# The one added to the decay's tanh in the RWKV projections: from VectorE's instruction to a second ScalarE activation in place

## The chip, the cores and the metric

The kernel runs on one core of a Trainium2 chip. The metric is the device time of one execution in microseconds (us), as the median of several runs. TensorE (PE, with its weight loads PEld), VectorE (DVE), ScalarE (ACT), GpSimd (POOL) and the DMA queues issued by SyncE (SP) work side by side; each engine runs its own instructions strictly in the order in which they stand in its list.

## The reference, cut to what matters

One layer of a hybrid encoder, 2048 tokens of 1024 numbers. The token mixer has attention heads and bidirectional RWKV heads over one shared projection, and then 16 experts follow. The piece that the change touches is the decay `w` of the RWKV heads, for each of two directions:

```
p = _centred_shift(p, mu_shift)
r, k, v, dw, da, dg = jnp.split(p, ...)
tw = jnp.tanh(dw)
...
w = jnp.exp(-DECAY_SCALE * jax.nn.sigmoid(w0[d] + tw @ w_up[d]))
a = jax.nn.sigmoid(a0[d] + da @ a_up[d])
kd = heads(k * (1.0 + (a - 1.0) * k_a))
```

The kernel has no sigmoid: it uses sigmoid(z) = (tanh(z/2) + 1)/2. So the logarithm of the decay needs `u = tanh(z/2) + 1`, and the running sums of `u` over chunks of tokens give all decay products.

## The kernel before, in words

The program has three stages: projections (`phase1`, to about 760 us), the mixers (RWKV and attention as two interleaved streams, to about 2250 us), and the output projection with the experts (to the end).

`phase1` works through two halves of 1024 tokens. In each half, a hand-written order calls pieces: four `heads(ct)` pieces h0 to h3 (128 RWKV channels each), four query/key pieces q0 to q3, one value piece, and, in the first half, the early loading of the next half's x. A heads piece projects r, k and v by `shifted`, and then `prep` makes what the mixers need of them.

- `project` makes one product: 24 matmuls (L247) of 258 columns into one PSUM bank of a pool `p1_pj` with 3 banks. `shifted` follows it with ACT's first tap (L263) and two DVE taps (L265) that add the left and right neighbours. PE gets the bank back only when the second DVE tap is done.
- `prep` goes over 2 stretches of 512 tokens and 2 directions d, that is 32 times in the whole of `phase1`. Each time: PE's low-rank products (L385), ACT's tanh `u` (L388) and tanh `a` (L389), **the one that is added to `u` (L390)**, DVE's scan `cum` (L392), exponentials on ACT (L394, L404 to L406), and products on DVE and POOL (L397 to L416) into a tile `X` that goes out by DMA. `a` and `u` have one buffer each, so the next tanh `a` (L389) waits until DVE's L414 has read the last one.
- `load_piece` prepares x for the projections: DVE copies `ht` (L195), and `split` (ACT L148, DVE or POOL L149) divides it into the two parts `hh` and `hl`. The query/key pieces put L324 to L329 on DVE.

The order of instructions on each engine is not written by hand below the level of pieces: the framework's scheduler places all instructions of all pieces by its own planned times, with `high_priority` for the taps. An instruction that is put on another engine can therefore move others, up to the mixers.

Of the kernel before, what the change touches and what calls it, by code (L numbers as in the profile page):

```python
# [11 lines left out]
AF = mybir.ActivationFunctionType  # L12
ALU = mybir.AluOpType
# [24 lines left out]
class Encoder:  # L38
# [317 lines left out]
    def prep(self, half, ct, rkv, lora, rates, sg):  # L356

        nc, ps, tpool = self.nc, self.ps, self.tpool
        tt, ts, stt, act = nc.vector.tensor_tensor, nc.vector.tensor_scalar, nc.vector.scalar_tensor_tensor, nc.scalar.activation
# [9 lines left out]
        for q in range(2):  # L369
            qs = slice(q * 512, (q + 1) * 512)  # L370
            t0 = half * HT + q * 512
            c0 = t0 // CH
            r, k, v = rkv[0][q], rkv[1][q], rkv[2][q]
            tl = lambda tag, bufs=None: tpool.tile([P, 512], F32, tag=tag, name=tag, bufs=bufs)
            self.to_tokens(v, self.d_v[t0 : t0 + 512, cs_])
            pb = self.spread(rt, q)
            kk = tl("kkn", 2)
            stt(out=kk, in0=k, scalar=self.kkh[:, ct : ct + 1], in1=pb, op0=ALU.mult, op1=ALU.mult)
            kds = []
            for d in range(2):  # L380
                pp = []
                for m in range(2):
                    pm = ps.tile([P, 512], F32, tag="ps", name="lora_ps")
                    for i in range(2):
                        nc.tensor.matmul(pm, lora[m][i][:, d, :], rates[m][:, qs], start=(i == 0), stop=(i == 1))  # L385
                    pp.append(pm)
                u, a = tl("u"), tl("a")
                act(out=u, in_=pp[0], func=AF.Tanh, bias=self.w0h[:, 4 * d + ct : 4 * d + ct + 1], scale=0.5)  # L388
                act(out=a, in_=pp[1], func=AF.Tanh, bias=self.a0h[:, 4 * d + ct : 4 * d + ct + 1], scale=0.5)  # L389
                nc.vector.tensor_scalar(out=u, in0=u, scalar1=1.0, scalar2=None, op0=ALU.add)  # L390
                cum = tl("cum")
                nc.vector.tensor_tensor_scan(out=cum, data0=self.cmask, data1=u, initial=0.0, op0=ALU.mult, op1=ALU.add)  # L392
                last = c3(cum)[:, :, CH - 1 : CH]
                act(out=self.pc[:, d, ct, c0 : c0 + 8], in_=last.rearrange("p c o -> p (c o)"), func=AF.Exp, scale=-0.5 * DSC)  # L394
                ex = tl("ex")
                if d == 0:
                    tt(out=ex, in0=cum, in1=u, op=ALU.subtract)  # L397
                    inc = cum
                else:
                    tt(out=c3(ex), in0=last.to_broadcast([P, 8, CH]), in1=c3(cum), op=ALU.subtract)  # L400
                    inc = u
                    tt(out=inc, in0=ex, in1=u, op=ALU.add)
                pinv = tl("pinv")
                act(out=pinv, in_=inc, func=AF.Exp, scale=0.5 * DSC)  # L404
                act(out=ex, in_=ex, func=AF.Exp, scale=-0.5 * DSC)
                act(out=inc, in_=inc, func=AF.Exp, scale=-0.5 * DSC)  # L406
                X = tpool.tile([P, 4, 512], F32, tag="X", name="X", bufs=2)
                bk = X[:, :, 0:256].rearrange("p c (u x t) -> p c u x t", u=2, x=2)
                stt(out=X[:, :, 256:384], in0=c2(kk), scalar=-2.0, in1=c2(ex), op0=ALU.mult, op1=ALU.mult)
                gt(out=X[:, :, 384:512], in0=c2(r), in1=c2(inc), op=ALU.mult)  # L410
                kd = tl(f"kd{d}")
                act(out=kd, in_=a, func=AF.Identity, scale=self.kah[:, ct : ct + 1], bias=self.kah1[:, ct : ct + 1])
                stt(out=a, in0=a, scalar=1.0, in1=kk, op0=ALU.add, op1=ALU.mult)
                tt(out=bk[:, :, :, 0, :], in0=c4(a), in1=c4(pinv), op=ALU.mult)  # L414
                gt(out=kd, in0=kd, in1=k, op=ALU.mult)
                tt(out=bk[:, :, :, 1, :], in0=c4(kd), in1=c4(pinv), op=ALU.mult)  # L416
                kds.append(kd)
                nc.sync.dma_start(out=self.d_x[d, ct, :, c0 // 2 : c0 // 2 + 4, :], in_=X)

            gt(out=kds[0], in0=kds[0], in1=kds[1], op=ALU.add)  # L420
            br = tl("pinv")
            stt(out=br, in0=r, scalar=self.rk[:, ct : ct + 1], in1=kds[0], op0=ALU.mult, op1=ALU.mult)
            pbo = ps.tile([P, 512], F32, tag="ps", name="pbo")
            nc.tensor.matmul(pbo, self.bblk, br, start=True, stop=True)
            bv = tl("cum")
            tt(out=bv, in0=pbo, in1=v, op=ALU.mult)
            pg = ps.tile([P, 512], F32, tag="ps", name="pg")
            nc.tensor.matmul(pg, self.g_l[:, cs_], sg[:, qs], start=True, stop=True)
            gl = tl("ex")
            act(out=gl, in_=pg, func=AF.Copy, scale=self.lnw[:, ct : ct + 1])  # L430
            nc.sync.dma_start(out=self.d_gl[ct, :, t0 : t0 + 512], in_=gl)
            stt(out=bv, in0=bv, scalar=self.lnb[:, ct : ct + 1], in1=pg, op0=ALU.add, op1=ALU.mult)
            nc.sync.dma_start(out=self.d_bg[ct, :, t0 : t0 + 512], in_=bv)
# [1181 lines left out]
```

## Time and profile before

| | before |
|---|---|
| median of 3 runs (lowest, highest) | 3757.07 us (3744.38, 3762.44) |
| the profiled execution: its time, its span | 3751.49 us, 3749.8 us |
| mean granted TensorE clock, share of full speed | 0.957 |
| busy in the whole span: PE, DVE, ACT, POOL | 94%, 67%, 47%, 40% |
| busy in 125 to 355 us (first half's heads): PE, DVE, ACT, POOL | 208.5, 193.1, 115.2, 108.8 of 230 us |

The shares of the whole span are means over three stages that are bound by different engines; the lowest row is from the stage in which the changed instruction runs. Times in the rows below are microseconds from the span's start, and means of one instruction are in nanoseconds (ns).

### The profile page before, as it was taken

To read this page: it belongs to the slowest core of one execution; us is meant where nothing else is said; L and a number is where in the kernel's file an instruction comes from. 1 tells how busy PE (TensorE), PEld (TensorE's weight loads), DVE (VectorE), ACT (ScalarE), POOL (GpSimd) and SP (SyncE) were. 2 spreads that over 40 slices of the span, in tenths; PEclk is the share of its full clock that TensorE was granted. 3 is DMA by queue.
4 is the path that set the end of the run, shared out by engine and by line. 5 is a ranking of instruction groups with operands and counts; after the bars stand their busy time and mean duration, and the time that the engine had idled before them with its cause. 6 is when DMAs were issued, how large, how long until landed. Compare 5 with 4: busy or idle time off the path is not lost. (4 is left out here: it accounts for less than half of the span.)

```text
span 3749.8 us, 61495 instructions
## 1 busy us (share of the span) xinstructions
PE 3509.9 (94%) x23436; PEld 2856.7 (76%) x23436; DVE 2516.7 (67%) x4289; ACT 1755.2 (47%) x3066; POOL 1512.5 (40%) x1484
## 2 busy tenths in 40 slices
PE   6998899799999999999999997993999999999998
PEld 5887788656666666676666664772999999999997
DVE  6688778876857778558867675447555656655653
ACT  4445444414555555545555564231444444444443
POOL 3445344526263353663364554332332332322321
PEclk8999899879999999999999998996999999999999
DMA  5335334443323433433333232443566766767664
GB/s 182 105 130 168 112 113 141 139 129 73 91 68 79 121 95 85 114 88 87 84 85 85 69 82 82 156 145 113 188 206 205 222 202 216 218 203 222 220 199 127
DMA packets 531228, 510.93 MB, mean 136 GB/s; under 512 B 213304, under 2 KB 449954, under 8 KB 525812
## 3 DMA queue, kind: packets, MB, share of 16 engines
q1 hardware_dynamic: 520612, 472.08, 41.1%
q0 software_dynamic: 10000, 34.91, 4.0%
q8 instruction: 185, 3.03, 0.3%
q14 instruction: 111, 0.91, 0.1%
q10 hardware_dynamic: 320, 0.00, 0.0%
HBM read 392.57 MB, written 109.07 MB: 134 GB/s over the span
## 5 line engine op out<-in xcount | busy, mean ns | idle before, releaser
L1452 DVE TENSOR_TENSOR w_lo<-w_raw,w_hi 128x2048 fp32r<-128x2048 f32 x189 | 432.3, 2293 | 385.8 <-ACT w_hi L1449 385.4
L1516 PE MATMUL gu<-hh,w_lo 128*128 128x256 f32 x2048 | 573.5, 280 | 0.0
L1516 PE MATMUL gu<-hl,w_hi 128*128 128x256 f32 x2048 | 572.7, 280 | 0.0
L1516 PE MATMUL gu<-hh,w_hi 128*128 128x256 f32 x2048 | 572.5, 280 | 0.0
L699 POOL TENSOR_TENSOR acc<-acc,pt 128x512 f32<-128x512 f32 x256 | 354.9, 1391 | 469.0 <-ACT pt L696 456.0
L1449 ACT CAST w_hi<-w_raw 128x2048 fp32r<-128x2048 f32 x192 | 366.9, 1912 | 319.9 <-PE down L1539 133.3
L696 ACT ACTIVATE pt<-st_ps 128x1024 f32<-128x1024 f32 x256 | 262.2, 1024 | 394.8 <-PE st_ps L695 221.2
L649 DVE TENSOR_REDUCE mx<-s_ps 128x1 f32<-128x512 f32 x512 | 342.6, 681 | 149.7 <-PE s_ps L648 148.2
L247 PE MATMUL proj_ps<-hh,w_hi 128*128 128x258 f32 (+1 forms) x1280 | 375.3, 294 | 32.8 <-DVE s_k L265 23.8
L1516 PEld LDWEIGHTS gu<-hh,w_lo 128*128 128x128 f32 x2048 | 388.0, 189 | 0.0
L1516 PEld LDWEIGHTS gu<-hh,w_hi 128*128 128x128 f32 x2048 | 385.6, 188 | 1.3
L1516 PEld LDWEIGHTS gu<-hl,w_hi 128*128 128x128 f32 x2048 | 385.5, 188 | 1.4
L247 PE MATMUL proj_ps<-hl,w_hi 128*128 128x258 f32 (+1 forms) x1280 | 373.0, 292 | 6.4 <-DVE hl L149 5.9
L247 PE MATMUL proj_ps<-hh,w_lo 128*128 128x258 f32 (+1 forms) x1280 | 371.5, 290 | 0.0
L149 POOL TENSOR_TENSOR dl<-hid,dh 128x256 fp32r<-128x256 f32 x128 | 135.1, 1056 | 448.1 <-ACT dh L148 447.8
L686 PE MATMUL o_ps<-pt,av 128*64 128x512 f32 x1024 | 278.5, 627 | 6.7 <-ACT pt L696 6.7
L247 PEld LDWEIGHTS proj_ps<-hh,w_hi 128*128 128x128 f32 x1280 | 250.8, 196 | 41.7 <-issue 23.0
L247 PEld LDWEIGHTS proj_ps<-hl,w_hi 128*128 128x128 f32 x1280 | 251.4, 196 | 10.6 <-DVE hl L149 6.6
L699 DVE TENSOR_TENSOR acc<-acc,pt 128x512 f32<-128x512 f32 x192 | 194.7, 1014 | 91.0 <-ACT pt L696 90.3
L247 PEld LDWEIGHTS proj_ps<-hh,w_lo 128*128 128x128 f32 x1280 | 250.6, 196 | 2.1 <-issue 1.1
L647 PE MATMUL s_ps<-khh,qhl 128*128 128x512 f32 x512 | 240.6, 471 | 9.5 <-DVE mx L649 8.1
L694 PE MATMUL st_ps<-qhl,khh 128*128 128x512 f32 x512 | 229.0, 447 | 2.8 <-ACT pt L696 1.8
(418 smaller groups left out, 8125.1 us busy)
## 6 DMA issues: line engine op xcount, KB each, us to landing
w_raw<-in_w_gate_dram SPq DMA_DIRECT2D x64, 1024.0 KB
w_raw<-in_w_up_e_dram SPq DMA_DIRECT2D x64, 1024.0 KB
w_raw<-in_w_down_dram SPq DMA_DIRECT2D x64, 1024.0 KB
d_x<-X SPq DMA_DIRECT2D x32, 1024.0 KB
xin<-d_x SPq DMA_DIRECT2D x64, 512.0 KB
w_raw<-in_w_in_dram SPq DMA_DIRECT2D x80, 256.0 KB
mod_w<-in_w_ada_dram SPq DMA_DIRECT2D x64, 256.0 KB
mod_w<-in_w_ada_dram SPq DMA_DIRECT2D x8, 1024.0 KB
```

Of the source, the lines that this page charges most:

```text
L149: (eng or nc.gpsimd).tensor_tensor(out=lo, in0=src, in1=hi.bitcast(F32), op=ALU.subtract)
L247: nc.tensor.matmul(acc[:, :n], a[:, kt, :], b[:, kt, lo : lo + n], start=(kt == 0 and m == 0), stop=(kt == KT - 1 and m == 2))
L647: nc.tensor.matmul(s, qs[h][:, ts], khh[:, ks], start=True, stop=False)
L649: nc.vector.tensor_reduce(out=mx[:, 4 * h + qt, kc : kc + 1], in_=s, axis=AX.X, op=ALU.max)
L686: nc.tensor.matmul(av[64 * h : 64 * h + 64, :], v[:, kb, :], pt[:, h, :], start=(kb == 0), stop=(kb == 15), tile_position=(0, 64 * h))
L694: nc.tensor.matmul(s[:, h, :], khh[:, ks], qs[h], start=True, stop=False)
L696: nc.scalar.activation(out=pt, in_=s, func=AF.Exp, scale=0.125)
L699: eng.tensor_tensor(out=acc[:, h, :], in0=(first if kb == 1 else acc)[:, h, :], in1=pt[:, h, :], op=ALU.add)
L1449: nc.scalar.copy(out=hi, in_=raw)
L1452: eng.tensor_tensor(out=lo, in0=raw, in1=hi.bitcast(F32), op=ALU.subtract)
L1516: nc.tensor.matmul(acc[:, m, :], a[:, kt, i * P : (i + 1) * P], b[:, kt, :], start=(kt == 0 and n == 0), stop=(kt == KT - 1 and n == 2))
```

## The change

```diff
                 u, a = tl("u"), tl("a")
                 act(out=u, in_=pp[0], func=AF.Tanh, ...)
                 act(out=a, in_=pp[1], func=AF.Tanh, ...)
-                nc.vector.tensor_scalar(out=u, in0=u, scalar1=1.0, scalar2=None, op0=ALU.add)
+                act(out=u, in_=u, func=AF.Identity, bias=1.0)
                 cum = tl("cum")
                 nc.vector.tensor_tensor_scan(out=cum, data0=self.cmask, data1=u, ...)
```

DVE loses 32 instructions and ACT gets 32. Both read and write the same tile of 128 x 512 numbers in place. The new one carries its bias and scale as constants in the instruction, while the two tanhs read their bias from a tile. All other instructions are the same, but their order on each engine is planned anew. Three places follow, with a minus for a row's place before and a plus for its place now.

On DVE, in the first half, about 176 to 183 us: the heads piece h1 (`s_k` is its k projection, L265 its taps) runs beside a query/key piece (`qk_t`, `qk_xn`).

```order
 L416 TENSOR_TENSOR X<-kd_1569,pinv 128x4x2x64
 L414 TENSOR_TENSOR X<-a,pinv 128x4x2x64
-L390 TENSOR_SCALAR u<-u 128x512
-L265 SCALAR_TENSOR_TENSOR s_k<-proj_ps,prm_ex,s_k 128x256
+L265 SCALAR_TENSOR_TENSOR s_k<-proj_ps,prm_ex,s_k 128x256 x2
 L328 TENSOR_TENSOR qk_t_1773<-qk_sq,rope_693 128x512
+L392 SCALAR_TENSOR_TENSOR cum<-cmask,u 128x512
 L324 SCALAR_TENSOR_TENSOR qk_xn<-p,qkn,pb 128x512
-L392 SCALAR_TENSOR_TENSOR cum<-cmask,u 128x512
-L265 SCALAR_TENSOR_TENSOR s_k<-proj_ps,prm_ex,s_k 128x256
 L329 TENSOR_TENSOR qk_t_1772<-qk_t_1772,qk_t_1773 128x512
```

The second tap has moved ahead of L328, L324 and the scan L392. The second half has the same change at the same piece.

On DVE again, about 240 to 250 us, the next heads piece's k projection:

```order
 L416 TENSOR_TENSOR X<-kd_2349,pinv 128x4x2x64
 L409 SCALAR_TENSOR_TENSOR X<-kkn,ex 128x4x128
+L265 SCALAR_TENSOR_TENSOR s_k<-proj_ps,prm_ex,s_k 128x256 x2
+L328 TENSOR_TENSOR qk_t_2553<-qk_sq,rope_693 128x512
 L265 SCALAR_TENSOR_TENSOR s_k<-proj_ps,prm_ex,s_k 128x256
-L390 TENSOR_SCALAR u<-u 128x512
 L413 SCALAR_TENSOR_TENSOR a<-a,kkn 128x512
 L392 SCALAR_TENSOR_TENSOR cum<-cmask,u 128x512
+L324 SCALAR_TENSOR_TENSOR qk_xn<-p,qkn,pb 128x512
+L329 TENSOR_TENSOR qk_t_2552<-qk_t_2552,qk_t_2553 128x512
 L265 SCALAR_TENSOR_TENSOR s_k<-proj_ps,prm_ex,s_k 128x256
-L328 TENSOR_TENSOR qk_t_2553<-qk_sq,rope_693 128x512
```

Three taps now stand ahead of L413 and L392, where one did.

On ACT, about 137 to 151 us, the second direction of the first `prep` (`p`, `qk_sq`: a query/key piece; `w_hi`: a weight of the next projection; `s_r`: the next heads piece's first tap):

```order
+L390 ACTIVATE u<-u 128x512
 L253 COPY p<-proj_ps 128x256
 L316 ACTIVATE qk_sq<-p 128x512
-L253 COPY p<-proj_ps 128x256
+L394 ACTIVATE pc<-cum 128x8
 L299 CAST hrt<-pn 128x256
+L253 COPY p<-proj_ps 128x256
 L148 CAST w_hi<-w_raw 128x512 x2
 L253 COPY p<-proj_ps 128x256
 L316 ACTIVATE qk_sq<-p 128x512
+L389 ACTIVATE a<-lora_ps,prm_ex 128x512
 L263 ACTIVATE s_r<-proj_ps,prm_ex 128x256
```

The tanh `a` (L389) now stands ahead of a first tap (L263), behind which it stood before.

## Rows read from the trace of the kernel before

**Rows 1.** The page's busy times of the whole span.
```profile
PE 3509.9 (94%) x23436; PEld 2856.7 (76%) x23436; DVE 2516.7 (67%) x4289; ACT 1755.2 (47%) x3066; POOL 1512.5 (40%) x1484
```

**Rows 2.** Windows: length, busy PE, PEld, DVE, ACT, POOL (instructions), clock, DMA share, GB/s.
```profile
125.00:355.00 230.00, 208.50 (x1604) 193.18 (x1603) 193.06 (x303) 115.18 (x238) 108.79 (x73) 0.96 0.39 135
355.00:425.00 70.00, 51.72 (x342) 43.43 (x341) 62.17 (x138) 41.17 (x87) 30.82 (x21) 0.80 0.49 159
...
475.00:720.00 245.00, 225.31 (x1730) 207.60 (x1728) 200.60 (x310) 116.52 (x238) 111.51 (x83) 0.97 0.37 128
720.00:860.00 140.00, 114.73 (x435) 74.18 (x436) 114.52 (x202) 33.56 (x51) 46.62 (x34) 0.70 0.48 128
860.00:2250.00 1390.00, 1358.96 (x8319) 947.75 (x8319) 995.59 (x1644) 775.92 (x1559) 702.22 (x808) 0.98 0.35 88
```

**Rows 3.** PE's long waits: start, length, instruction, idle before and releaser.
```profile
182.30 0.55 PE L247 MATMUL proj_ps<-hh,w_hi 128*128 128x258 f32 x1 [4.83 <-DVE s_k L265]
...
250.75 0.55 PE L247 MATMUL proj_ps<-hh,w_hi 128*128 128x258 f32 x1 [4.67 <-DVE s_k L265]
...
374.99 0.58 PE L247 MATMUL proj_ps<-hl,w_hi 128*128 128x256 f32 x1 [4.88 <-DVE hl L149]
...
533.28 0.55 PE L247 MATMUL proj_ps<-hh,w_hi 128*128 128x258 f32 x1 [4.81 <-DVE s_k L265]
...
601.75 0.55 PE L247 MATMUL proj_ps<-hh,w_hi 128*128 128x258 f32 x1 [4.67 <-DVE s_k L265]
```

**Rows 4.** Windows behind or around long waits, columns as in the second group.
```profile
181.10:187.80 6.70, 5.50 (x25) 5.53 (x26) 6.70 (x8) 1.62 (x4) 6.70 (x4) 0.50 0.45 146
...
372.30:396.00 23.70, 12.44 (x61) 9.62 (x62) 23.41 (x50) 13.54 (x29) 11.92 (x8) 0.50 0.42 160
720.40:754.40 34.00, 20.47 (x66) 15.43 (x67) 32.84 (x41) 14.39 (x26) 21.27 (x13) 0.50 0.58 175
```

**Rows 5.** Groups by line, 0:800: busy us, mean ns | idle before, releaser.
```profile
L412 ACT ACTIVATE kd<-a,prm_ex 128x512 f32<-128x512 f32 x32 | 26.0, 814 | 0.4
...
L405 ACT ACTIVATE ex<-ex 128x512 f32<-128x512 f32 x32 | 20.0, 626 | 8.2 <-DVE ex L397 8.2
...
L390 DVE TENSOR_SCALAR u<-u 128x512 f32<-128x512 f32 x32 | 18.7, 584 | 9.1 <-ACT u L388 8.9
```

**Rows 6.** The changed line's instructions: ns, shortest/median/longest, first and last start.
```profile
L390 DVE TENSOR_SCALAR u<-u x32: 410/427/1497, 132.8 to 734.1; 128x512 f32<-128x512 f32 x32
```

**Rows 7.** Waits, 100:760: who <- whom: us in total, times, longest us.
```profile
PE proj_ps L247 <- DVE s_k L265: 23.8, 8, 4.8
...
ACT a L389 <- DVE X L414: 23.5, 13, 3.4
...
DVE u L390 <- ACT u L388: 8.9, 11, 1.7
```

**Rows 8.** ACT's timeline, 173.7:178.6, columns as in the third group.
```profile
174.00 0.40 ACT L148 CAST l_hi<-l_raw 128x256 fp32r<-128x256 f32 x1
177.82 0.69 ACT L389 ACTIVATE a<-lora_ps,prm_ex 128x512 f32<-128x512 f32 x1 [3.42 <-DVE X L414]
```

**Rows 9.** DVE's timeline, 177.8:182.1.
```profile
177.71 0.42 DVE L390 TENSOR_SCALAR u<-u 128x512 f32<-128x512 f32 x1
178.05 0.47 DVE L265 SCALAR_TENSOR_TENSOR s_k<-proj_ps,prm_ex,s_k 128x256 f32<-128x256 f32 x1
178.44 0.67 DVE L328 TENSOR_TENSOR qk_t<-qk_sq,rope 128x512 f32<-128x512 f32 x1
...
179.70 2.08 DVE L392 TENSOR_TENSOR_SCAN cum<-cmask,u 128x512 f32<-128x512 bf16 x1
181.70 0.45 DVE L265 SCALAR_TENSOR_TENSOR s_k<-proj_ps,prm_ex,s_k 128x256 f32<-128x256 f32 x1
```

**Rows 10.** DVE's timeline, 242.4:250.5.
```profile
242.34 0.47 DVE L265 SCALAR_TENSOR_TENSOR s_k<-proj_ps,prm_ex,s_k 128x256 f32<-128x256 f32 x1
...
250.13 0.47 DVE L265 SCALAR_TENSOR_TENSOR s_k<-proj_ps,prm_ex,s_k 128x256 f32<-128x256 f32 x1
```

## The prediction

> **What bounds the kernel now.** I looked at the page first: PE is busy in 94% of the span and every other engine is far below [rows 1]. That share says nothing of the stage that is changed, so the next view was the windows. In the mixers, 860 to 2250 us, PE is busy in 1359 of 1390 us; nothing is taken out there, and a shorter DVE list in the projections cannot shorten it. In the heads pieces it is otherwise: from 125 to 355 us PE is busy in 208.5 of 230 us and idle in 21.5, from 475 to 720 us it is idle in 19.7 of 245, and from 355 to 425 us it is idle in 18.3 of 70 with a clock of 0.80. DVE is the fuller of the others in each of these: 84%, 82% and 89%, against 50%, 48% and 59% for ACT [rows 2]. So the third view was PE's waits: the ones longer than 4 us in these stretches are for DVE, four times for the second tap L265, which gives a PSUM bank back, and once for `hl` of L149 [rows 3, 7]. What such a wait costs is more than itself: behind the one that ends at 182.30 the granted clock is 0.50 (1.2 instead of 2.4 GHz) for 6.7 us, though PE is nearly full there [rows 4]; 6.7 us at half speed lose 3.4 us. So in the projections DVE's queue sets when PE goes on, and ACT is the engine with room.
>
> **The change part by part.**
>
> *Removed from DVE.* 32 instructions, 18.7 us in all, 584 ns in the mean [rows 5]; the median is 427 ns and the longest 1497 [rows 6], so the mean holds some that ran against other traffic, and 32 x 427 ns = 13.7 us is the lower bound of what leaves DVE's queue. I take 18.7, since it is the sum of what did run.
>
> *Added to ACT.* The trace has no Identity with constant bias in SBUF. The nearest rows are L405, an Exp of the same shape in place with no operand from a tile, 626 ns, and L412, an Identity of the same shape with two operands from a tile, 814 ns [rows 5]. That bounds 32 of them by 20.0 and 26.0 us; I take 626 ns, since L405 is the one with the same operands, 20.0 us in all. In the two heads stretches ACT is idle for 115 and 128 us [rows 2], so 20 us find room in time. Whether they find it at the right moment is a matter of places: at 174.40 ACT waits 3.42 us with nothing to do until L389 may start [rows 8], and the new order puts an L390 just there, ahead of the waiting one. This is cover of the best kind. Without cover 0.63 us would go into the scan's way each time.
>
> One rule speaks against the move: the Trainium skill, "ScalarE: Activation LUTs", section "Rules for kernel authors", says of adds and multiplies to use VectorE and not ScalarE, since VectorE is faster per element; the rows agree on the single instruction, 427 against 626 ns [rows 5, 6]. What it would do if it decided is the fourth rival below.
>
> *Moved.* Three places carry the result, and in all three a tap or a piece of x gets out from behind other DVE work.
> - About 178 us, and again in the second half: before, one tap ends at 178.52, then L328, L324 and the scan run, and the second tap ends at 182.15; PE starts at 182.30 [rows 3, 9]. In the new order both taps stand together, so the second ends about 178.5: 3.6 us of the 4.8 go, twice (PE's wait at 533.28 is the same) = 7.2 us.
> - About 250 us, and again at 601.75: before, the tap that releases PE ends at 250.60 [rows 10]; its work on PE is long done. In the new order it is the third tap, with one L328 between them, from 242.34 on: 3 x 0.47 + 0.67 = 2.1 us [rows 9, 10], so it ends about 244.4, some 6 us earlier, more than the whole wait of 4.67 us. Twice 4.67 = 9.3 us, and the half clock behind each goes as well, 2 x 3.4 = 6.7 us [rows 3, 4].
> - 374.99 us: PE waits 4.88 us for `hl` [rows 3]. The new order has L195 and L149 of the next half's x ahead of the scan and the products of h3's `prep`, so this goes too: 4.9 us.
>
> Together 7.2 + 9.3 + 6.7 + 4.9 = 28.1 us. But most of this is reordering: what was behind the taps is still to be done, DVE is 84% busy, and what is put off comes back as a wait elsewhere unless DVE truly has less to do. What it has less to do is 18.7 us. So I take **18.7 us** as the gain and 28.1 as a bound.
>
> *Late next.* Behind the taps come the scan and the products into X; they feed DMA and the mixers, which begin only after 760 us. At that hand-over, 720 to 754 us, DVE is busy in 32.8 of 34 us and PE in 20.5 at a clock of 0.50 [rows 4]. Here too DVE is the one awaited; its work there changes place by a few instructions, which I count as nothing, with 10 us either way in the range.
>
> *Sum.* The profiled execution took 3751.5 us (its span 3749.8 and 1.7 around it). 3751.5 - 18.7 = 3732.8. This execution lies 5.6 us below the median of the three runs; half of that towards the median makes **3735 us**.
>
> **The rivals.**
>
> 1. *Swallowed.* PE gets its banks earlier but then waits for something that has not moved: a weight cast on ACT, the low-rank products, or at the end of the stage the hand-over. For it: PE has some 40 us of idle in the two heads stretches, of which only 19 are in the four tap waits [rows 2, 3]; the rest is spread in small pieces over many causes. Against it: DVE is the fullest of the others throughout. The time: 3745 to 3757, no change.
>
> 2. *Slower: ACT's queue blocks PE's banks.* ACT's tanh `a` (L389) waits for DVE's L414, 13 times for 23.5 us, the longest 3.4 [rows 7]. What stands behind it on ACT waits too. In the new order L389 stands ahead of a first tap (L263) or a weight cast (L148) at some seven places where it stood behind, as the rows for ACT in the section on the change show for one. A first tap that is late holds a bank, and PE with it: at most 3.4 us and 3.4 of half clock behind it, 6.8 us a place. Seven make 47.6 us: 3751.5 - 18.7 + 47.6 = 3780. It takes three places to undo the gain (18.7 / 6.8 = 2.75) and six to be slower by 18.8 us. Against it: DVE is to come to L414 earlier, and 13 waits average 1.8 us.
>
> 3. *Scan path longer.* In 11 of 32 cases DVE already sat idle for tanh `u`, 8.9 us in all [rows 7]. In those the scan would start later by the tanh `a` ahead of the new instruction and by the difference of the two instructions, 0.69 + 0.63 - 0.43 = 0.9 us [rows 5, 6, 8]; 11 times that is 9.8 us if nothing else fills DVE and nothing gains: 3761.
>
> 4. *The slower engine counts.* If ACT's time weighed as DVE's does, the price is 32 x (626 - 427) ns = 6.4 us: 3758. ACT is half idle [rows 2], so this has little for it. It is what the Trainium skill's rule above would come to.
>
> **How the numbers follow.** A measurement of this kernel tells a change of about 0.5% (18.8 us) from none: below 3738.3 is faster and above 3775.9 slower, by the median of before. My forecast (gain of 10 to 28 us) 0.47, of which 0.36 lies below 3738.3, since the forecast is close to that bound; a larger relief, with the 28.1 us and half of the 23.7 us at half clock around 375 us [rows 4] returned, 3751.5 - 28.1 - 11.9 = 3711.5 and down to 3705 with the hand-over, 0.12; swallowed 0.18; ACT's queue 0.13, of which 0.11 slower; scan path 0.06; the slower engine 0.04. So faster 0.48, same 0.41, slower 0.11. The range goes from 3706, the end of the larger relief, to 3770, which is rival 3 (3761) with the 10 us of the hand-over against it; what is left out is most of rival 2 and a little of the larger relief, about 0.15. The forecast case alone would be 3722 to 3745.
>
> **What would show it.** In the profile of the changed kernel: L390 on ACT, 32 times near 626 ns; DVE's busy time in the heads stretches down by about 9 us each; PE's waits at the four taps gone or below 1.5 us, and with two of them the 0.50 behind them; the wait for `hl` near 375 us gone; the mixers' length, 1390 us, unchanged. I am wrong if PE's waits for ACT's L263 or for weights grow by as much as those for L265 shrink (rival 1), if ACT's waits at L389 for L414 grow and PE's banks with them (rival 2), if DVE's idle time before the scan L392 grows by about 10 us (rival 3), or if the mixers take another time than before, which nothing here prices.

## The result, and the profile after

The changed kernel takes 3773.08 us (median of 10 runs, 3755.30 to 3790.89) against 3748.78 us of the kernel before in the same measurement (10 runs): a ratio of 1.0054, with a 95% interval of 1.0037 to 1.0072. By the ratio it is slower by some 20 us (by the medians 24); the forecast was 18.7 us faster, and 3773 lies above the range. Its profiled execution took 3777.57 us.

The page's busy times [rows 1] have hardly moved: DVE has 29.5 us less, ACT 15.9 more, and PE 24.2 more, with the same number of instructions.

```profile
PE 3534.1 (94%) x23436; PEld 2865.9 (76%) x23436; DVE 2487.2 (66%) x4257; ACT 1771.1 (47%) x3098; POOL 1521.5 (40%) x1484
```

What was moved looks much as priced. The view of the changed line (shortest, median, longest, in ns):

```profile
L390 ACT ACTIVATE u<-u x32: 617/634/662, 132.5 to 726.8; 128x512 f32<-128x512 f32 x32
```

Its group by line, with the sum:

```profile
L390 ACT ACTIVATE u<-u 128x512 f32<-128x512 f32 x32 | 20.3, 636 | 0.2
```

32 instructions, 20.3 us, within 617 to 662 ns, where the DVE instruction went from 410 to 1497 [rows 6]. In the kernel before, the 15 of them that started while no GpSimd instruction was running took 410 to 427 ns; of the 17 that started beside one, 12 took 549 ns and more. The Trainium skill, "ScalarE: Activation LUTs", section "What ACT_TABLE_LOAD costs", gives 186 ns + 0.833 ns per element for such an instruction, so an estimate of 612 ns; the trace agrees within 4%.

In the two heads stretches [rows 2] DVE is busy 5.1 and 5.8 us less (about 9 each were forecast), and PE is idle 17.4 and 19.7 us instead of 21.5 and 19.7. Windows of the changed kernel, the last one its mixers from the first RWKV product (L955) to the output projection:

```profile
125.00:355.00 230.00, 212.62 (x1618) 195.52 (x1617) 187.97 (x297) 122.98 (x255) 112.49 (x74) 0.95 0.42 140
475.00:720.00 245.00, 225.26 (x1753) 206.68 (x1752) 194.81 (x310) 130.70 (x265) 120.52 (x87) 0.98 0.40 137
...
787.00:2327.00 1540.00, 1481.58 (x8734) 1015.47 (x8732) 1079.42 (x1817) 823.48 (x1639) 746.92 (x839) 0.96 0.34 85
```

The same stage of the kernel before:

```profile
799.00:2300.00 1501.00, 1452.27 (x8726) 998.95 (x8725) 1083.32 (x1814) 822.00 (x1638) 741.04 (x838) 0.97 0.35 87
```

The mixers begin 12 us earlier than before, at 787 instead of 799 us, and end 27 us later. They take 1540 us instead of 1501, although nothing in them was edited. Of the 39 us, 10 are idle time of PE (1540 - 1481.6 = 58.4 against 48.7), and 29 are PE being busy longer over the same instructions, at a lower granted clock. What did change there is the order in which the instructions stand: of 5736 PE instructions of the mixers (as the program lists them) 4762 stand at another position, of 1893 DVE instructions 1519.

Each window is of one execution, and executions differ. The mixers of run 1 below stand in the order of the kernel before, and yet its profiled execution, 14 us above the median of its kernel, has them at 1525 us and 0.96; other executions of that same order have 1509 (run 3) and 1497 (run 7):

```profile
787.00:2312.00 1525.00, 1469.07 (x8721) 1014.07 (x8718) 1083.84 (x1813) 821.83 (x1638) 746.10 (x838) 0.96 0.34 85
```

So what the order is worth is not read from a pair of windows but from the medians of runs 1 and 2.

PE's waits in the projections [rows 3, 7] did not go as forecast either. Waits of the changed kernel, 100 to 760 us (who <- whom: us in total, times, longest):

```profile
ACT a L389 <- DVE X L414: 30.8, 13, 3.9
...
PE proj_ps L247 <- DVE s_k L265: 24.0, 12, 4.0
...
DVE cum L392 <- ACT u L390: 4.3, 3, 1.4
...
PE proj_ps L247 <- DVE hl L149: 3.7, 1, 3.7
```

The timeline of PE has the five waits at the places that answer to [rows 3]:

```profile
184.36 0.55 PE L247 MATMUL proj_ps<-hh,w_hi 128*128 128x258 f32 x1 [3.97 <-DVE s_k L265]
...
249.28 0.36 PE L247 MATMUL proj_ps<-hh,w_hi 128*128 128x258 f32 x1 [2.35 <-DVE s_k L265]
...
387.00 0.38 PE L247 MATMUL proj_ps<-hl,w_hi 128*128 128x256 f32 x1 [3.70 <-DVE hl L149]
...
536.36 0.36 PE L247 MATMUL proj_ps<-hh,w_hi 128*128 128x258 f32 x1 [4.00 <-DVE s_k L265]
...
600.67 0.36 PE L247 MATMUL proj_ps<-hh,w_hi 128*128 128x258 f32 x1 [2.36 <-DVE s_k L265]
```

The sum of the waits for the taps is 24.0 us, as before (23.8), in 12 pieces instead of 8. The first of the five shows why. Ahead of it PE's timeline has a short wait that the two taps ended which now stand together:

```profile
177.25 0.36 PE L247 MATMUL proj_ps<-hh,w_hi 128*128 128x258 f32 x1 [1.48 <-DVE s_k L265]
```

DVE's timeline in the changed kernel, from that pair to the tap that ends the wait of 3.97 us:

```profile
176.12 0.99 DVE L265 SCALAR_TENSOR_TENSOR s_k<-proj_ps,prm_ex,s_k 128x256 f32<-128x256 f32 x2
...
180.41 1.74 DVE L413 SCALAR_TENSOR_TENSOR a<-a,kkn 128x512 f32<-128x512 f32 x1
182.07 0.47 DVE L265 SCALAR_TENSOR_TENSOR s_k<-proj_ps,prm_ex,s_k 128x256 f32<-128x256 f32 x1
182.47 1.35 DVE L400 TENSOR_TENSOR ex<-cum 128x512 f32<-128x512 f32 x1
183.74 0.47 DVE L265 SCALAR_TENSOR_TENSOR s_k<-proj_ps,prm_ex,s_k 128x256 f32<-128x256 f32 x1
```

The pair is done at 177.1, even before the forecast 178.5. PE runs one more product with the bank that this frees, and then waits for the tap at 183.74, which stands behind the scan L392 and the products that had been put off.

### The profile page after: what moved, and what is told of

The parts are those of the page before. It is cut to its first block, busy times and chain, and to the rows that moved or that the text cites. A ratio compares the mean times of both kernels' runs of the same rounds, so it can differ in the third digit from the quotient of the medians.

```text
span 3775.7 us, 61473 instructions
## 1 busy us (share of the span) xinstructions
PE 3534.1 (94%) x23436; PEld 2865.9 (76%) x23436; DVE 2487.2 (66%) x4257; ACT 1771.1 (47%) x3098; POOL 1521.5 (40%) x1484
## 5 line engine op out<-in xcount | busy, mean ns | idle before, releaser
L649 DVE TENSOR_REDUCE mx<-s_ps 128x1 f32<-128x512 f32 x512 | 343.3, 681 | 171.3 <-PE s_ps L648 169.1
L247 PE MATMUL proj_ps<-hh,w_hi 128*128 128x258 f32 (+1 forms) x1280 | 373.8, 293 | 31.1 <-DVE s_k L265 24.0
L247 PE MATMUL proj_ps<-hl,w_hi 128*128 128x258 f32 (+1 forms) x1280 | 370.7, 290 | 4.7 <-DVE hl L149 3.7
L247 PE MATMUL proj_ps<-hh,w_lo 128*128 128x258 f32 (+1 forms) x1280 | 369.4, 289 | 0.0
L247 PEld LDWEIGHTS proj_ps<-hh,w_hi 128*128 128x128 f32 x1280 | 248.5, 194 | 39.5 <-issue 27.3
L699 DVE TENSOR_TENSOR acc<-acc,pt 128x512 f32<-128x512 f32 x192 | 179.7, 936 | 118.8 <-ACT pt L696 117.8
L247 PEld LDWEIGHTS proj_ps<-hl,w_hi 128*128 128x128 f32 x1280 | 249.2, 195 | 9.4 <-DVE hl L149 3.9
L247 PEld LDWEIGHTS proj_ps<-hh,w_lo 128*128 128x128 f32 x1280 | 248.5, 194 | 1.9 <-issue 0.6
```

The source lines that it names most:

```text
L247: nc.tensor.matmul(acc[:, :n], a[:, kt, :], b[:, kt, lo : lo + n], start=(kt == 0 and m == 0), stop=(kt == KT - 1 and m == 2))
L649: nc.vector.tensor_reduce(out=mx[:, 4 * h + qt, kc : kc + 1], in_=s, axis=AX.X, op=ALU.max)
L699: eng.tensor_tensor(out=acc[:, h, :], in0=(first if kb == 1 else acc)[:, h, :], in1=pt[:, h, :], op=ALU.add)
```

## The experiments

After the result the theory was: **the order of the mixers decides**. The projections gained some 10 us, and the planner, which places all stages by its own planned times, dealt the mixers a worse order. The rival: the mixers are slower because they start earlier or because of the move itself, and their order does not matter.

To tell these apart, a kernel must be built with an order that is chosen, not planned. All pinned kernels add this one function, with a list of instruction numbers for each engine; it adds edges of issue order between neighbours of the list and no wait:

```
+def pin_order(tc):
+    at = {i.name: i for i in tc.nc.cur_bb.bb.instructions}
+    info = mybir.DependencyInfo(mybir.DependencyClass.NoSync, mybir.DependencyReason.DATA)
...
+            if last is not None and last.engine == ins.engine:
+                tc.add_manual_dep(ins, last.name, info, reason="pinned")
+            last = ins
```

With the two orders of the projections, the two orders of the mixers, and the one on either engine, this makes a table of which four cells were built beside the two kernels. The expectations count from 3749 us for the kernel before. It was measured anew with each group of runs, at 3756.58 us for runs 1 to 4, 3749.62 for 5, 6, 8 and 9, and 3757.14 for the others, so expectation and measurement are compared by their distance from it.

**1. moved_mix_of_before**: the changed kernel and

```
+    pin_order(tc)   # PINNED: the mixers of the kernel before, all five engines
```

> The changed kernel (the one is added on ACT, projections in their new order), with each engine's instructions of the mixers kept in the order of the kernel before. Theory (the order of the mixers decides: the projections gained about 10 us, the mixers lost about 36 by their new order): 3749 - 10 = about 3739 us, 3733 to 3745. Rival (the mixers are slower because they start some 10 us earlier, against other transfers, or by anything else that the move itself does; their order is not what matters): as the changed kernel, about 3773 us.

Measured: 3748.83 us against 3756.58, ratio 0.9977 (0.9960 to 0.9994). The loss is gone with the order, and about 8.6 us of gain are left (2 to 15 by the interval; 10 were expected). Its mixers begin at 787 us, as early as those of the changed kernel, so the early start is not what makes them slower.

**2. kept_mix_of_after**: the kernel before and

```
+    pin_order(tc)   # PINNED: the mixers of the changed kernel
```

> The kernel before (the one is added on DVE, projections in their old order), with the mixers' instructions in the order of the changed kernel. Theory (order of the mixers): 3749 + 25 to 36 = 3774 to 3785 us. Rival (start time or the move itself): as the kernel before, about 3749 us.

Measured: 3786.55 us, ratio 1.0083 (1.0056 to 1.0110), 31 us slower than the kernel before without a single other change. The first two runs agree: the changed order costs 0.83% with the old projections and 1.0054 - 0.9977 = 0.77% with the new ones. That is what the theory expected (25 to 36 us more). The window over the mixers of run 2 is as long as that of the changed kernel:

```profile
795.00:2335.00 1540.00, 1478.69 (x8729) 1012.46 (x8728) 1080.47 (x1814) 821.52 (x1638) 750.04 (x838) 0.96 0.34 85
```

**3. moved_orders_of_before**: the changed kernel and

```
+    pin_order(tc)   # PINNED: the whole program in the order of the kernel before, L390 free
```

> The move alone: the one is added on ACT, but every other instruction of all engines stays in the order of the kernel before. Theory (order of the mixers): not slower, and what DVE's shorter queue gives by itself, 0 to 10 us, so 3739 to 3749 us; the prediction's term of 18.7 us for the queue would give 3730. Rival (the move itself makes the mixers slower): about 3773 us.

Measured: 3751.20 us, ratio 0.9995 (0.9975 to 1.0015). The move by itself can't be told from no change, as the theory's 0 to 10 us of gain allow; 18.7 us (0.9950) are outside the interval. In its trace the mixers begin 8 us earlier than before, at 791 us, and end at the same 2300 us; PE's first long wait is shorter, 3.29 us instead of 4.83 [rows 3]:

```profile
179.88 0.55 PE L247 MATMUL proj_ps<-hh,w_hi 128*128 128x258 f32 x1 [3.29 <-DVE s_k L265]
```

So the queue is shorter and PE does go on earlier, as the prediction had it, but less than half of the 18.7 us reach the mixers.

**4. kept_proj_of_after**: the kernel before and

```
+    pin_order(tc)   # PINNED: projections of the changed kernel, mixers of the kernel before
```

> The new order of the projections without the move: the one is added on DVE, projections in the order of the changed kernel, mixers in the order of the kernel before. If the 10 us that the projections gained come from the order of the taps: 3739 us. If they come from the instructions that left DVE: 3749 us or a little above, since DVE has its 18.7 us back. Either way the theory expects no loss in the mixers, and the rival none either, since nothing is moved to ACT.

Measured: 3775.06 us, ratio 1.0054 (1.0033 to 1.0075), 20 us slower. Neither expectation held: the new order of the projections, without the move, costs 20 us, and the move on top of it (run 1) takes them away and 8.6 more. Its profiled execution, at 3761.19 us the shortest of its ten, shows one price of it at the hand-over, a wait of PE for the first load of the mixers:

```profile
754.93 0.58 PE L846 MATMUL p<-xin 64*128 64x128 f32 x1 [14.66 <-DMA xin<-d_x]
```

In the kernel before, the timeline has a wait of 3.44 us for such a load, and in run 1, whose instructions stand in the same order on PE, the first of these products starts at 713.1 us, 42 us earlier, without such a wait:

```profile
724.35 0.58 PE L846 MATMUL p<-xin 64*128 64x128 f32 x1 [3.44 <-DMA xin<-d_x]
```

The loads wait for X, whose products stand on DVE; an order planned for a DVE with less to do fits badly once the instructions are back. That is an argument and not a measurement: what else belongs to the 20 us is open.

The six kernels side by side:

| projections in the order | mixers in the order | the one on | ratio |
|---|---|---|---|
| before | before | DVE | 1 (kernel before) |
| changed | changed | ACT | 1.0054 (changed kernel) |
| changed | before | ACT | 0.9977 (run 1) |
| before | changed | DVE | 1.0083 (run 2) |
| before | before | ACT | 0.9995 (run 3) |
| changed | before | DVE | 1.0054 (run 4) |

**5 and 6. half_d0, half_d1**: half of the change each, every order planned freely.

```
+                if d == 0:      # half_d1: d == 1
+                    act(out=u, in_=u, func=AF.Identity, bias=1.0)
+                else:
+                    nc.vector.tensor_scalar(out=u, in0=u, scalar1=1.0, scalar2=None, op0=ALU.add)
```

> Half of the change: the one is added on ACT for direction 0 (16 of 32), on DVE for direction 1, all orders planned freely. The mixers come out almost in the order of the kernel before (112 of 5736 PE instructions stand elsewhere). Theory (order of the mixers decides): not slower, 3745 to 3757 us where the kernel before takes 3750 to 3757. Rival (each one moved to ACT costs something): half of the change's 0.54%, some 10 us above the kernel before.

Measured: 3745.79 us against 3749.62, ratio 0.9986 (0.9969 to 1.0004), as the theory had it; the rival's 10 us more lie outside.

> The other half: the one is added on ACT for direction 1 (16 of 32), on DVE for direction 0, all orders planned freely. The mixers come out in an order that is near that of the changed kernel (their second half nearly the same, 45 of 2885 PE instructions elsewhere, their first half not). Theory (order of the mixers decides): slower by 0.4 to 0.9%, as with the whole change or more, about 3770 to 3787 us. Rival (each one moved costs something): half of the change's 0.54%, as half_d0.

Measured: 3793.33 us, ratio 1.0093 (1.0062 to 1.0123). Half of the change costs as much as the whole or more (the two intervals overlap between 1.0062 and 1.0072), and the other half nothing. Windows over the mixers of half_d0 and of half_d1:

```profile
794.00:2287.00 1493.00, 1441.40 (x8730) 990.49 (x8729) 1079.81 (x1815) 821.52 (x1639) 742.91 (x839) 0.98 0.35 87
```

```profile
798.00:2354.00 1556.00, 1494.51 (x8730) 1025.95 (x8728) 1083.73 (x1815) 824.34 (x1639) 749.95 (x839) 0.95 0.34 84
```

From the one to the other the mixers grow by 63 us: PE's idle time by 9.9 us (51.6 to 61.5), its busy time over the same 8730 instructions by 53.1. ACT, DVE and POOL are busy equally long within 1%. By the medians the kernels differ by 48 us, so single executions add to this: that of half_d0 is 9 us under its median, that of half_d1 12 above. In this pair the waits are the smaller part and the longer busy time at a lower clock (0.95 against 0.98) the larger. How much of the clock's part belongs to the order, and how much to the execution, the windows do not tell; run 10 shows it for one place.

**7. half_d1_mix_of_before**: half_d1 with the mixers pinned as in run 1.

```
+    pin_order(tc)   # PINNED: the mixers of the kernel before
```

> half_d1 (the one on ACT for direction 1 alone, 0.93% slower than the kernel before) with the mixers kept in the order of the kernel before; its projections stay in half_d1's own order. Theory (order of the mixers decides): the whole loss goes, 3745 to 3757 us, ratio 0.997 to 1.002. Rival (the projections' new order or the move makes the loss): as half_d1, about 3790 us.

Measured: 3755.89 us against 3757.14, ratio 0.9993 (0.9972 to 1.0014). The whole 0.93% is gone. The window over its mixers:

```profile
798.00:2295.00 1497.00, 1444.94 (x8730) 992.87 (x8728) 1083.64 (x1815) 823.32 (x1639) 745.79 (x839) 0.98 0.35 87
```

**8 and 9. kept_first_of_after, kept_second_of_after**: the kernel before with one half of the mixers in the changed order.

```
+    pin_order(tc)   # PINNED: first half of the mixers as changed, second as before; and the reverse
```

> The kernel before with the first half of the mixers (by the program's text, to about 1560 us) in the order of the changed kernel, the second half in its own. With the whole of the mixers in the changed order it was 31 us slower. If the loss stands in one stretch (the trace shows 17 of 38 us lost between 1050 and 1400): about +18 us, 3774. If the loss comes from nothing but disturbing an order that happened to be good, by about the number of instructions moved: about +15.

Measured: 3768.06 us against 3749.62, ratio 1.0045 (1.0027 to 1.0063), 17 us slower. The two expectations, 18 and 15 us, lie too close to be told apart.

> The kernel before with the second half of the mixers in the order of the changed kernel, the first half in its own. If the losses add: 31 less what the first half alone costs, 12 to 15 us, about 3770. If the first half carries all: as the kernel before, about 3755.

Measured: 3760.29 us, ratio 1.0020 (1.0001 to 1.0039). That is 7.5 us, between the two expectations, and barely clear of nothing. The two losses make 0.65%, within the interval of the whole (0.56 to 1.10%). So the first half carries a part of the loss and the second probably the rest; which part is the larger the two intervals, which overlap, leave open.

**10. kept_first_to_1470**: one place of it. In the changed order DVE's L649, the row maximum that gives PE a PSUM bank of the attention back, stands at about 1490 us behind five of DVE's other instructions. DVE's timeline in the changed kernel (a row with x2 is two instructions):

```profile
1489.47 0.34 DVE L876 TENSOR_TENSOR ts_t<-ts 64x184 f32<-64x184 f32 x1
1489.84 0.34 DVE L878 TENSOR_TENSOR ts<-ts,ts_t 64x184 f32<-64x184 f32 x1
1490.22 0.36 DVE L876 TENSOR_TENSOR ts_t<-ts 64x198 f32<-64x198 f32 x1
1490.50 0.68 DVE L699 TENSOR_TENSOR acc<-acc,pt 128x512 f32<-128x512 f32 x1
1491.11 0.88 DVE L878 TENSOR_TENSOR ts<-ts,ts_t 64x198 f32<-64x198 f32 x1
1491.91 1.27 DVE L649 TENSOR_REDUCE mx<-s_ps 128x1 f32<-128x512 f32 x2
```

PE's timeline there:

```profile
1490.15 0.49 PE L694 MATMUL st_ps<-qhl,khh 128*128 128x512 f32 x1
1492.64 0.50 PE L647 MATMUL s_ps<-khh,qhl 128*128 128x512 f32 x1 [2.00 <-DVE mx L649]
```

The window from there:

```profile
1492.60:1503.50 10.90, 10.86 (x61) 8.69 (x62) 6.13 (x17) 3.81 (x9) 0.00 (x0) 0.53 0.24 59
```

A wait of 2.00 us, and then PE is full for 10.9 us at 0.53. Before the wait PE was full as well, at 1.00:

```profile
1478.00:1490.60 12.60, 12.60 (x75) 8.67 (x73) 12.22 (x24) 10.12 (x20) 7.69 (x7) 1.00 0.16 53
```

In the kernel before, at the same step, DVE's L649 and the RWKV pieces alternate:

```profile
1480.64 0.30 DVE L876 TENSOR_TENSOR ts_t<-ts 64x150 f32<-64x150 f32 x1
1480.87 0.67 DVE L649 TENSOR_REDUCE mx<-s_ps 128x1 f32<-128x512 f32 x1
1481.47 0.29 DVE L878 TENSOR_TENSOR ts<-ts,ts_t 64x150 f32<-64x150 f32 x1
1481.69 0.67 DVE L649 TENSOR_REDUCE mx<-s_ps 128x1 f32<-128x512 f32 x1
```

and the window around it:

```profile
1478.00:1489.00 11.00, 9.71 (x72) 7.58 (x71) 10.63 (x28) 7.49 (x19) 1.77 (x2) 1.00 0.27 73
```

PE's idle time is 1.29 us in these 11 us (11.00 - 9.71), of which 0.89 is the wait for L649, and the clock stays at 1.00. The new kernel takes back the order of the kernel before from about 1470 us on:

```
-    pin_order(tc)   # PINNED: the changed order up to about 1560 us
+    pin_order(tc)   # PINNED: the changed order up to about 1470 us
```

> kept_first_of_after with its boundary moved forward from about 1560 us to about 1470: between the two, the order of the kernel before. The traces with the changed order all lose some 6.6 us at one place there (about 1490 us, where DVE's L649 stands behind five of its others, PE waits 2.0 us for it and runs at 0.50 for 7 to 10 us). Theory: in the profile that step is gone while those before it stay, and the time is some 6 us under kept_first_of_after, 3760 to 3764. Rival (the step has another cause than the order there): the step stays.

Measured: 3764.27 us against 3757.14, ratio 1.0020 (0.9999 to 1.0041), less than run 8 but not apart from it by the intervals. The trace decides by the step itself. Two neighbouring steps of the RWKV stream, first and last start of L955's four instructions (durations in ns, then the two times), in the kernel before:

```profile
L955 PE MATMUL av_ps<-ident,al x4: 272/276/282, 1488.8 to 1506.5; 128*128 128x128 f32 x4
```

the changed kernel:

```profile
L955 PE MATMUL av_ps<-ident,al x4: 273/350/421, 1497.3 to 1521.7; 128*128 128x128 f32 x4
```

kept_first_of_after:

```profile
L955 PE MATMUL av_ps<-ident,al x4: 273/350/421, 1500.4 to 1524.9; 128*128 128x128 f32 x4
```

and kept_first_to_1470:

```profile
L955 PE MATMUL av_ps<-ident,al x4: 272/276/280, 1495.0 to 1512.6; 128*128 128x128 f32 x4
```

17.7 us, 24.4, 24.5, and 17.6; run 2 has 24.2 and run 3 17.7. The step costs 6.5 to 6.9 us in all three traces that have the changed order there, and nothing where it doesn't stand. What lies before the step stays, as expected: from the first L955 to it run 10 takes 708 us, the kernel before 689, run 8 716.

**11 and 12. split_on_dve, split_mix_of_before**: does it need ACT at all? The one stays on DVE, in two instructions of half the width.

```
+                for x in (0, 256):
+                    nc.vector.tensor_scalar(out=u[:, x : x + 256], in0=u[:, x : x + 256], scalar1=1.0, scalar2=None, op0=ALU.add)
```

> Nothing goes to ACT: the one is added on DVE as before, but in two instructions of 256 columns each. That changes the planner's times a little, and 2435 of 5736 PE instructions of the mixers stand elsewhere than before. Direct price: 32 more DVE instructions, some 0.1 to 0.2 us each, 3 to 6 us. Theory (any small change of the projections' plan deals the mixers a new order, and the order decides): a time anywhere between some 5 us below and 40 us above the kernel before, to be read together with the next run. Rival (only the move to ACT costs): 0 to 6 us above the kernel before.

Measured: 3766.96 us against 3757.14, ratio 1.0029 (1.0005 to 1.0053).

> split_on_dve with the mixers kept in the order of the kernel before. Theory: 0 to 6 us above the kernel before, whatever split_on_dve takes; the difference of the two is the new order's price. Rival: the same as split_on_dve.

Measured: 3761.04 us, ratio 1.0011 (0.9986 to 1.0037). Both lie where the theory has them, but its range of 45 us could hardly have been missed, the two intervals overlap, and the rival's range of 0 to 6 us (up to 1.0016) reaches into both: inconclusive. The direct price came out as expected, two halves of 287 ns (median) for one instruction of 427, 32 times 147 ns = 4.7 us.

## Why the prediction was wrong

**The step that failed** is in its first part: "nothing is taken out there, and a shorter DVE list in the projections cannot shorten it", with the mixers' 1390 us expected "unchanged" and the other case left as one "which nothing here prices". The argument took the mixers' instructions, which are the same, for the mixers' order, which is not. Their new order costs 0.77 to 0.83%, 29 to 31 us (runs 1 and 2). Of the rivals none was this one. The order had been named as a thing that the change moves "up to the mixers"; that it had a price was left out of sum, range and chances. Only the signs of being wrong name it.

**The term of 18.7 us** was mis-sized as well. The mechanism stands: the taps L265 hold PE's banks, and a shorter DVE queue lets PE go on. The last products of the projections, PE's L247 (durations in ns, then first and last start), in the kernel before, the changed kernel and run 3:

```profile
L247 PE MATMUL proj_ps<-hh,w_lo x1280: 276/282/683, 39.0 to 714.4; 128*128 128x258 f32 x129, 128*128 128x256 f32 x54
```

```profile
L247 PE MATMUL proj_ps<-hh,w_lo x1280: 276/282/561, 39.1 to 703.7; 128*128 128x258 f32 x129, 128*128 128x256 f32 x54
```

```profile
L247 PE MATMUL proj_ps<-hh,w_lo x1280: 276/282/683, 39.2 to 705.8; 128*128 128x258 f32 x129, 128*128 128x256 f32 x54
```

The projections gain 10.7 us, by the move alone 8.6. A single trace is no closer than some 4 us: run 8, whose projections are as before, has this start at 710.2. (The start of the mixers is a worse measure, since their own order moves it too: 784 us in run 8, 799 before.) At the end 8.6 us arrive (run 1; 2 to 15), and by the move alone 2 (run 3; between 9 faster and 6 slower). 18.7 lies outside both intervals. With run 1's 8.6 us of gain and run 2's 31 us of loss the sum would have been some 22 us slower, and 20 were measured.

**The places.** At 182.30 and 533.28 the waits were to lose 3.6 us and lost 0.86 and 0.81; at 250.75 and 601.75 they were to go and fell from 4.67 to 2.35; at 374.99 the wait for `hl` was to go, and one of 3.70 us stands 12 us later. The taps moved ahead as forecast, and some ended even earlier, but the prediction followed each bank to the next product only: PE came back to wait for the taps behind the work that had been put off, 12 waits in place of 8, with the same sum. It was right to take the 28.1 us of reordering as a bound and not as the gain: the new order of the projections with the old instructions is 20 us slower (run 4).

**ACT's price** was right: 636 ns for a forecast of 626. It is hidden; the move in the old order shows no loss (run 3). The Trainium skill's rule for adds, in "ScalarE: Activation LUTs", section "Rules for kernel authors", speaks against the move; its reason, up to about three times the speed per element, is given there for bf16. The tiles here are f32, at 427 ns on DVE and 634 on ACT (medians). The fourth rival's loss of 6.4 us is not seen: run 3's interval ends at 5.6 us.

**The rivals.** *ACT's queue blocks PE's banks*: the waits of L389 for L414 did grow, from 23.5 to 30.8 us, but the same projections with the old order of the mixers are not slower (run 1), so this is not where the 20 us are. *Scan path longer*: its sign came, since DVE's idle time before the scan grew by 15 us. Groups by line, 0:800, before and changed (busy us, mean ns, then idle before):

```profile
L392 DVE TENSOR_TENSOR_SCAN cum<-cmask,u 128x512 f32<-128x512 bf16 x32 | 46.0, 1438 | 6.9 <-DMA d_bg<-cum 5.0 <-POOL X L410 1.5
```

```profile
L392 DVE TENSOR_TENSOR_SCAN cum<-cmask,u 128x512 f32<-128x512 bf16 x32 | 45.3, 1415 | 21.7 <-POOL X L410 9.8 <-DMA d_bg<-cum 4.8 <-ACT u L390 4.3
```

But 9.1 us of idle stood before L390 [rows 5], so the path had 16.0 us of idle before and has 21.7 now, of which 4.3 are for the one. Run 1 has the same 21.9 and is not slower, so this is not where the 20 us are either. *Swallowed*: partly so, as the waits in the projections show. The forecast landed on the wrong side by something that none of them names.

**What stays open**: which of the moved instructions carry the loss. One place was shown (6.5 to 6.9 us of some 30), and the losses of the halves add up to the whole. The orders of single engines were not exchanged alone, since each engine's order rests on the others'. The clock shares in a loss that differs from execution to execution, as the windows of one order show (1497 to 1525 us). And the kernel before was not pinned to its own order; runs 3 and 7, pinned and not slower (0.9995, 0.9993), speak against a price of the pinning itself.

## What to carry to other kernels

Where a planner places the whole program, an edit's direct price is only one term. Compare the order of all stages before and after, not that of the edited one alone, and leave room in the forecast for a new order: here the order of the mixers alone cost 31 us (run 2), more than any term of the edit. To learn what an edit itself is worth, keep the order of the rest fixed; and where a good order was found, keep it: pinned, the same change is 0.23% faster than the kernel before instead of 0.54% slower, the fastest by ratio of all that were measured, though its interval (0.9960 to 0.9994) overlaps those of runs 3 and 5.

## What the runs showed of the hardware

A short wait can cost several times its length. PE had been full at a granted clock of 1.00 for the 12.6 us up to 1490.6. Behind the wait of 2.00 us that ends at 1492.64 it is busy for 10.86 of 10.90 us at 0.53; an estimate from these numbers, 10.9 x 0.47 = 5.1 us, is most of the 6.5 to 6.9 that this step costs. At the same step of the kernel before the wait is 0.89 us, and the clock stays at 1.00.

Over the whole of the mixers the windows above, of single executions, differ in PE's idle time by 13 us at most (48.7 to 61.5) and in PE's busy time over the same instructions by 53. Not all of it is the order: the kernel before and run 1, with the mixers in one order, differ by 17 us in busy time (1452.3 and 1469.1).

The time of an instruction on VectorE went with what ran on GpSimd: in the kernel before the same addition took 410 to 427 ns with no GpSimd instruction running at its start, and up to 1497 with one. On ScalarE all 32 took 617 to 662.
